# Two pairs of weight buffers change places in memory: the a22 quarter of the feed-forward projection

## The chip, the core and the metric

The kernel runs on one core of one Trainium2 chip. The metric is the device time of one execution in microseconds, the median over repeated runs.

## What is computed

A decoder block over 512 positions of 1024 channels, float32 throughout. The part that matters here is its last stage, a gated feed-forward layer with a short causal convolution (`h` is 512 x 1024, `w_ffn_in` 1024 x 5632, `w_ffn_out` 2816 x 1024):

```python
h = rmsnorm(x, norm2_g[l])
gu = h @ w_ffn_in[l]
g = causal_dwconv(gu[..., :D_FF], ffn_conv_w[l]) + ffn_conv_b[l]
x = x + (jax.nn.silu(g) * gu[..., D_FF:]) @ w_ffn_out[l]
```

Ahead of it stand the input projection, a gated short convolution, sparse attention, and the merge through `w_o`. The change touches none of them.

## The kernel before

**Split operands.** Each float32 operand of a large product is held as a high part (the value in TensorE's reduced float32 format) and a low part (the rest). A product is then three matmuls per 128 x 128 block of weights: high x high, high weights x low data, low weights x high data. The helper `dense` issues, for each block, the two with the high weights (lines 437 and 438), and after all blocks those with the low weights (line 440). So a high buffer is loaded into TensorE twice for each block, a low one once.

**The feed-forward stage.** The 2816 columns are taken two tiles of 128 at a time (f = 0, 2, ..., 20, 11 pairs), each for the gate half (n = 0) and the up half (n = 1) of `w_ffn_in`: 22 calls of `ff_forms` and `ff_pair`. Each is a 2 x 2 block product by Strassen's scheme in Winograd's form: seven products instead of eight. The weights of a call are cut in four quarters a11, a12, a21, a22, each 128 columns by 512 channels (four blocks of 128 x 128). The data is cut likewise, and its seven forms (B11, T4, B21, B22, T1, T3, T2) are made once and kept in `xf_h` and `xf_l`, 256 positions each. Every one of the seven products thus has four blocks and 4 x 3 = 12 matmuls of 256 moving columns, eight with high weights and four with low.

**Where the weights of the seven products lie.** a11 and a12 are kept in a ring of tiles `wh`/`wl` (named wh_s and wl_s in the profile). The four sums of quarters are made on VectorE and split into `sh`/`sl`. a22 itself has its own small tiles: `th` (high) and `tl` (low), 128 partitions x 2048 bytes, two buffers each, used by turns. `ff_forms` fills them with `dma_split` (lines 171 to 175): ScalarE writes the rounded raw weights into th and their negative into tl, and a transfer on the POOL queue adds the weights from the chip's main memory into tl. Only the product with the data form T4 uses a22 (`product(b45[:, lo], "a22", T4)`): eight matmuls with th, alternately on xf_h and xf_l, then four with tl on xf_h. It is written first of the seven.

Between the calls, the parts of the product with `w_ffn_out` (`pdn` in the profile, weights wh_d and wl_d from the same ring, data `ah` and `al`) are put in, with 512 moving columns. The last one is cut in two of 256 columns.

**What sets the order and the places.** A scheduler sets the order of the instructions on each engine. Places in a partition's memory follow from the order in which a pool's tiles are first named: each tag gets its buffers behind those of the tag before. In the pool `pw`, the line that the change touches names one tag ahead of a spacer of 192 bytes, `gap_w`. The other tags follow as `ff_forms` first names them. In the built program the places are, in bytes from the start of each partition:

| tile | before | past a multiple of 512 |
| --- | --- | --- |
| xf_h (28,672 bytes) | 37,152 | 288 |
| xf_l (28,672 bytes) | 65,824 | 288 |
| th, two buffers | 94,496 and 96,544 | 288 |
| gap_w | 98,592 | |
| tl, two buffers | 98,784 and 100,832 | 480 |
| sums, sh, sl (behind tl) | 102,880 to 135,648 | 480 |
| ah, al | 138,720 to 167,392 | 480 |
| ring wh, wl | 204,768 to 229,344 | 480 |

Each further block of weights lies 512 bytes on, each further block of data 7,168 (14 x 512).

Of the kernel before, what the change touches and what calls it, by code (L numbers as in the profile page):

```python
# [12 lines left out]
F32R = mybir.dt.float32r  # L13
# [5 lines left out]
P = 128  # L19
D = 1024  # L20
# [65 lines left out]
def tile_block(ctx: ExitStack, tc: tile.TileContext, xT, pos, par, par2, w_tok, w_a3, w_gate, w_ao, w_bo, w_o,  # L86
# [13 lines left out]
    def const(shape, name, dt=F32, pool=sb):  # L100
        return pool.tile(shape, dt, name=name, tag=name)
# [798 lines left out]
    xf_h = const([P, 4, 7, TH], "xf_h", F32R, px)  # L900
    xf_l = const([P, 4, 7, TH], "xf_l", F32R, px)
    pw = ctx.enter_context(tc.tile_pool(name="pw", bufs=1, side="left"))
    pw.tile([P, D // 2], F32R, name="th_", tag="th", bufs=2)
    const([P, 48], "gap_w", F32, pw)

    def x_forms(k, v):
# [283 lines left out]
```

## Time and profile before

| | |
| --- | --- |
| median of 3 runs | 697.33 us (697.29 to 697.89) |
| profiled execution, its own time | 696.92 us |
| its span, first to last instruction | 695.1 us |
| TensorE (PE) busy | 689.2 us, 99% |
| weight loads (PEld) busy, beside PE | 614.5 us, 88% |
| VectorE (DVE) busy | 511.7 us, 74% |
| ScalarE (ACT) busy | 436.7 us, 63% |
| GpSimd (POOL) busy | 248.7 us, 36% |

The profile is of one execution. A group's row gives line, engine, operation, the tile written and those read, the shape, the count, and behind the bar the busy time in us, the mean of one in ns, and the idle time of the engine ahead of them. Matmuls are pipelined: a record's duration runs from its issue to its modelled end and overlaps with the next. The pace of TensorE is the time from one start to the next.

### The profile page before, as it was taken

What the parts mean: (1) busy time and instruction counts of PE and PEld (TensorE: products, weight loads), DVE (VectorE), ACT (ScalarE), POOL (GpSimd) and SP (SyncE); (2) the same over time, 40 slices, a digit from 0 to 9 for tenths busy, and PEclk for the clock granted to TensorE, in tenths of its full rate; (3) what the DMA queues carried; (4) which work ended last, traced back from release to release, by engine and by line L of the source; (5) the groups of instructions that cost most, each with busy time, mean ns of one, the idle gap of its engine ahead of it and who ended that gap; (6) DMA issues with size and microseconds to landing.
All of it is one profiled execution on the core that took longest, in us unless ns stands there. A gap on an engine that the chain in (4) does not pass through costs nothing.

```text
span 695.1 us, 11268 instructions
## 1 busy us (share of the span) xinstructions
PE 689.2 (99%) x4111; PEld 614.5 (88%) x4111; DVE 511.7 (74%) x897; ACT 436.7 (63%) x776; POOL 248.7 (36%) x247
## 2 busy tenths in 40 slices
PE   9999999999999999999999999999999999999997
PEld 9999888887878888788889999999999999999986
DVE  6987886766566546475888999898787787877543
ACT  7635654878888866535776857665566655566530
POOL 4041443477788867462112212121122211112110
PEclk9999999999999999999999999999999999999999
DMA  8333686568666654563586977997877979775665
GB/s 268 113 98 122 170 194 145 132 240 237 222 222 228 195 169 124 193 229 118 130 198 160 219 192 167 245 218 180 215 173 180 210 172 227 174 175 112 132 137 152
DMA packets 57623, 124.87 MB, mean 180 GB/s; under 512 B 5344, under 2 KB 21088, under 8 KB 57568
## 3 DMA queue, kind: packets, MB, share of 16 engines
q1 hardware_dynamic: 35648, 79.39, 35.3%
q0 software_dynamic: 14848, 32.51, 27.4%
q10 hardware_dynamic: 7072, 12.26, 5.5%
q8 instruction: 32, 0.52, 0.3%
q14 instruction: 23, 0.19, 0.1%
HBM read 111.55 MB, written 12.58 MB: 179 GB/s over the span
## 4 chain that ended last, share of the span: by engine, by line
PE 95%; ACT 2%; DMA 1%; POOL 1%; DVE 1%; issue 0%; SPq 0%; ACTq 0%; POOLq 0%
PE p L438 10%; PE p L437 10%; PE p L440 10%; PE pdn L438 6%; PE pdn L437 6%; PE pdn L440 6%; PE pg L437 4%; PE pg L438 4%; PE pg L440 3%; PE pa L438 3%; PE pa L437 3%; PE pa L440 3%; PE po L438 2%; PE po L440 2%; PE po L437 2%; PE pj_s L269 2%
## 5 line engine op out<-in xcount | busy, mean ns | idle before, releaser
L437 PE MATMUL p<-xf_h,sh 128*128 128x256 f32 x336 | 80.6, 277 | 0.0
L438 PE MATMUL p<-xf_l,sh 128*128 128x256 f32 x336 | 80.5, 276 | 0.0
L175 POOL DMA_DIRECT2D wl_s<-in_w_ff_dram x22 | 19.6, 891 | 156.1 <-ACT wl_s L174 154.8
L438 PE MATMUL pdn<-al,wh_d 128*128 128x512 f32 (+1 forms) x176 | 68.5, 389 | 0.0
L437 PE MATMUL pdn<-ah,wh_d 128*128 128x512 f32 (+1 forms) x176 | 68.3, 389 | 0.0
L438 PEld LDWEIGHTS p<-xf_l,sh 128*128 128x128 f32 x336 | 63.1, 188 | 0.0
L437 PEld LDWEIGHTS p<-xf_h,sh 128*128 128x128 f32 x336 | 63.1, 188 | 0.0
L167 ACT ACTIVATE sh<-s 128x1024 fp32r<-128x1024 f32 x44 | 46.3, 1055 | 25.3 <-PE p L438 22.4
L168 DVE TENSOR_TENSOR sl<-s,sh 128x1024 fp32r<-128x1024 f32 x44 | 53.5, 1218 | 8.7 <-ACT sh L167 8.6
L173 ACT ACTIVATE wh_s<-wr_s 128x1024 fp32r<-128x1024 f32 x22 | 23.3, 1060 | 56.9 <-PE pdn L438 54.3
L750 POOL TENSOR_TENSOR tn_e<-tn_e,ph 128x512 fp32r<-128x512 f32 x40 | 51.2, 1294 | 16.2 <-ACT ph L749 16.0
L440 PE MATMUL p<-xf_h,sl 128*128 128x256 f32 x336 | 52.2, 277 | 0.0
L175 POOL DMA_DIRECT2D wl_d<-in_w_dn_dram x22 | 26.7, 1212 | 71.3 <-ACT wl_d L174 71.3
L437 PE MATMUL pg<-xg_h,wh_g 128*128 128x512 f32 x128 | 50.1, 392 | 0.0
L438 PE MATMUL pg<-xg_l,wh_g 128*128 128x512 f32 x128 | 50.1, 391 | 0.0
L440 PE MATMUL pdn<-ah,wl_d 128*128 128x512 f32 (+1 forms) x176 | 47.5, 388 | 0.0
L440 PEld LDWEIGHTS p<-xf_h,sl 128*128 128x128 f32 x336 | 44.7, 188 | 0.2
L1109 DVE TENSOR_TENSOR x<-x,pdn 128x512 f32<-128x512 f32 x47 | 32.0, 682 | 15.9 <-PE pdn L440 15.3
L150 POOL TENSOR_TENSOR wl_g<-wr_g,wh_g 128x1024 fp32r<-128x1024 f32 x16 | 38.5, 2405 | 10.4 <-ACT wh_g L148 9.7
L438 PE MATMUL p<-xf_l,wh_s 128*128 128x256 f32 x168 | 40.6, 277 | 0.0
L437 PE MATMUL p<-xf_h,wh_s 128*128 128x256 f32 x168 | 40.5, 277 | 0.0
L175 POOL DMA_DIRECT2D tl<-in_w_ff_dram x22 | 19.7, 894 | 57.3 <-ACT tl L174 49.7
(367 smaller groups left out, 2117.5 us busy)
## 6 DMA issues: line engine op xcount, KB each, us to landing
wr_s<-in_w_ff_dram SPq DMA_DIRECT2D x44, 512.0 KB, 5.0
wl_s<-in_w_ff_dram POOLq DMA_DIRECT2D x22, 512.0 KB, 7.8
wr_d<-in_w_dn_dram ACTq DMA_DIRECT2D x22, 512.0 KB, 8.3
wl_d<-in_w_dn_dram POOLq DMA_DIRECT2D x22, 512.0 KB, 9.0
wr_g<-in_w_gate_dram SPq DMA_DIRECT2D x16, 512.0 KB, 4.0
wr_a<-in_w_a_dram SPq DMA_DIRECT2D x12, 512.0 KB, 3.7
tl<-in_w_ff_dram POOLq DMA_DIRECT2D x22, 256.0 KB, 7.6
td_e<-e SPq DMA_DIRECT2D x16, 256.0 KB, 4.4
```

Source lines behind the costliest of these rows:

```text
L150: e.tensor_sub(lo[:, 0:n], raw[:, 0:n], hi[:, 0:n].bitcast(F32))
L167: hi = nc.scalar.activation(h, v, AF.Copy)
L168: nc.vector.tensor_sub(l, v, h.bitcast(F32))
L173: nc.scalar.activation(h, raw, AF.Copy)
L175: nc.gpsimd.dma_start(l if dst is None else dst, src, accum_op=ALU.add)
L269: nc.tensor.matmul(acc, xg_h[:, k, ts_], wh, start=k == 0, stop=False)
L437: ops.append(nc.tensor.matmul(acc, wh, xh, start=first and i == 0, stop=False))
L438: ops.append(nc.tensor.matmul(acc, wh, xl, start=False, stop=False))
L440: nc.tensor.matmul(acc, wl, xh, start=False, stop=last and i == len(units) - 1)
L750: nc.gpsimd.tensor_sub(pl, pt, ph.bitcast(F32))
L1109: nc.vector.tensor_add(xj, xj, acc)
```

## The change

One line names another tag ahead of the spacer, so that the low buffers are placed there and the high ones behind it:

```diff
     pw = ctx.enter_context(tc.tile_pool(name="pw", bufs=1, side="left"))
-    pw.tile([P, D // 2], F32R, name="th_", tag="th", bufs=2)
+    pw.tile([P, D // 2], F32R, name="tl_", tag="tl", bufs=2)
     const([P, 48], "gap_w", F32, pw)
```

In the built program th now lies at 98,784 and 100,832, and tl at 94,496 and 96,544. No other tile has another place. Every instruction, its order on its engine and its waits are the same as before.

## The prediction

> **What bounds the kernel now.** I read the page's busy table and its chain of waits first, then the waits of TensorE in the feed-forward stage, the only stage that uses the two buffers, then that stage's matmul groups, and at last single matmuls in order of time.
>
> ```profile
> span 695.1 us, 11268 instructions
> ...
> PE 689.2 (99%) x4111; PEld 614.5 (88%) x4111; DVE 511.7 (74%) x897; ACT 436.7 (63%) x776; POOL 248.7 (36%) x247
> ...
> PE 95%; ACT 2%; DMA 1%; POOL 1%; DVE 1%; issue 0%; SPq 0%; ACTq 0%; POOLq 0%
> ```
>
> TensorE is busy 99% of the span and the chain that ended last runs 95% through it. From 355 us to the end the list of waits for its weight loads has one row, and the list for its matmuls has none:
>
> ```profile
> PEld pdn7x L437 <- DVE x L1109: 0.3, 1, 0.3
> ```
>
> ```profile
> 440.00:690.00 250.00, 250.00 (x1731) 231.44 (x1731) 187.35 (x262) 138.54 (x181) 45.75 (x45) 1.00 0.78 179
> ```
>
> The second row gives the stretch, its length, and the busy time and count of PE, PEld, DVE, ACT and POOL: PE is busy 250.00 of 250.00 us at full clock. Nothing is waited for, so the stage lasts as long as its matmuls take to follow each other, and a nanosecond on the pace of one matmul reaches the end of the kernel. A nanosecond elsewhere reaches nothing.
>
> Within that stretch the groups of matmuls, one row per weight buffer (the last two numbers before the bar's end are busy us and mean ns of one):
>
> ```profile
> L437 PE MATMUL p<-xf_h,sh 128*128 128x256 f32 x240 | 57.4, 276 | 0.0
> ...
> L440 PE MATMUL p<-xf_h,sl 128*128 128x256 f32 x240 | 37.0, 276 | 0.0
> L437 PE MATMUL p<-xf_h,wh_s 128*128 128x256 f32 x120 | 28.7, 276 | 0.0
> ...
> L440 PE MATMUL p<-xf_h,wl_s 128*128 128x256 f32 x120 | 18.5, 276 | 0.0
> L438 PE MATMUL p<-xf_l,th 128*128 128x256 f32 x60 | 14.9, 282 | 0.0
> L437 PE MATMUL p<-xf_h,th 128*128 128x256 f32 x60 | 14.9, 281 | 0.0
> L440 PE MATMUL p<-xf_h,tl 128*128 128x256 f32 x60 | 9.2, 276 | 0.0
> ```
>
> All have one shape. Every weight buffer gives 276 ns, tl too, and th alone gives 281 and 282. These durations overlap, so the pace is read from starts. One a22 product and the product behind it, in order of time (start us, duration us):
>
> ```profile
> 488.98 0.28 PE L437 MATMUL p<-xf_h,th 128*128 128x256 f32 x1
> ...
> 489.81 0.28 PE L438 MATMUL p<-xf_l,th 128*128 128x256 f32 x1
> 489.93 0.62 PE L440 MATMUL p<-xf_h,tl 128*128 128x256 f32 x4
> 490.38 0.28 PE L437 MATMUL p<-xf_h,wh_s 128*128 128x256 f32 x1
> ...
> 491.18 0.28 PE L438 MATMUL p<-xf_l,wh_s 128*128 128x256 f32 x1
> 491.29 0.62 PE L440 MATMUL p<-xf_h,wl_s 128*128 128x256 f32 x4
> 491.74 0.28 PE L437 MATMUL p<-xf_h,wh_s 128*128 128x256 f32 x1
> ```
>
> The eight th matmuls take 489.93 - 488.98 = 0.95 us, 119 ns each. The four tl matmuls take 0.45 us, 113 each. Eight with wh_s take 0.91 and four with wl_s 0.45, again 113 each. So th costs about 0.04 us per product more than another buffer would, 5 ns a matmul, the same 5 ns as between 276 and 281 or 282. The slowness ends with the last th matmul: tl, behind it, is at pace at once.
>
> **Why th.** The addresses of the built program offer a reason. Both moving tiles, xf_h and xf_l, lie 288 bytes past a multiple of 512 bytes in their partition. So do both th buffers. Every other weight buffer of the stage, tl, sh, sl, wh and wl, lies 480 past one, because gap_w (192 bytes) stands behind th and ahead of the rest. A weight load streams while the matmul before it streams its moving operand, so equal offsets could make the two meet in the same part of the memory. One other place tests this, the last w_dn product, which is cut into two of 256 columns. There a moving tile (ah, al) and the weights (wh_d, wl_d) all lie 480 past a multiple of 512, as they do in the products of 512 columns ahead of it:
>
> ```profile
> 688.34 0.39 PE L437 MATMUL pdn<-ah,wh_d 128*128 128x512 f32 x1
> ...
> 689.02 0.39 PE L438 MATMUL pdn<-al,wh_d 128*128 128x512 f32 x1
> 689.25 0.62 PE L440 MATMUL pdn<-ah,wl_d 128*128 128x512 f32 x2
> 689.70 0.28 PE L437 MATMUL pdn<-ah,wh_d 128*128 128x256 f32 x1
> 689.81 0.28 PE L438 MATMUL pdn<-al,wh_d 128*128 128x256 f32 x1
> 689.93 0.28 PE L437 MATMUL pdn<-ah,wh_d 128*128 128x256 f32 x1
> 690.05 0.28 PE L438 MATMUL pdn<-al,wh_d 128*128 128x256 f32 x1
> 690.17 0.40 PE L440 MATMUL pdn<-ah,wl_d 128*128 128x256 f32 x2
> ```
>
> At 512 columns four take 689.25 - 688.34 = 0.91 us, 227 each, which is twice 113.5: no penalty. At 256 columns, from the second on, three take 690.17 - 689.81 = 0.36 us, 120 each: th's pace, with other buffers far from th. Equal offsets and 256 columns is what the two places share. It is an inference from two places, not a demonstration.
>
> **The change part by part.** It removes, adds and moves no instruction: the instructions and their waits stand in the same order on every engine. Four buffers get other addresses. th moves to 98,784 and 100,832 (480 past a multiple of 512), tl to 94,496 and 96,544 (288 past one). There are 22 such products (2 halves for each of 11 pairs of tiles).
>
> First term, th leaves the offset of its moving tiles: eight matmuls at 113.5 in place of 119, -0.04 us a product. Second term, tl takes that offset: four matmuls per product, all with xf_h. Its cost is not in the trace. From below it is nothing, since tl now runs at 113 beside the same xf_h and could go on so. From above it is th's own penalty on each, 4 x 5 = 0.02 us, or 4 x 6.5 = 0.026 at the 120 ns of the last product. A gain from the move is excluded: tl is already at the common pace. I take 0.02, because the equal offset is the nearest condition for which rows exist, and both rows of it pay. Net: -0.04 + 0.02 = -0.02 us a product.
>
> The count has its own bounds. Where the program takes several products by turns, the pace is 119 for buffers at any offset:
>
> ```profile
> 408.34 0.28 PE L437 MATMUL p<-xf_h,sh 128*128 128x256 f32 x1
> ...
> 409.17 0.28 PE L438 MATMUL p<-xf_l,sh 128*128 128x256 f32 x1
> 409.29 0.63 PE L440 MATMUL p<-xf_h,sl 128*128 128x256 f32 x4
> ```
>
> Eight sh matmuls take 0.95 us here, so a better offset would bring th nothing in such a stretch. Such stretches all lie ahead of 440 us; the means of 276 behind it leave no room for one. Behind 440 us are 60 / 4 = 15 products, which gain for certain if any do. So 15 to 22 products x 0.02 = 0.3 to 0.44 us, and I take 0.4. As the stage has no waits, all of it arrives at the end.
>
> Third term, the writers of the buffers. ScalarE writes th and tl, and a transfer from the POOL queue adds into tl. These are covered by lead time:
>
> ```profile
> 370.22 0.92 POOL L175 DMA_DIRECT2D tl<-in_w_ff_dram  x1 [1.24 <-ACT tl L174]
> ...
> 478.01 0.86 POOL L175 DMA_DIRECT2D tl<-in_w_ff_dram  x1
> ```
>
> ```profile
> 380.25 0.62 PE L440 MATMUL p<-xf_h,tl 128*128 128x256 f32 x4
> ...
> 504.95 0.62 PE L440 MATMUL p<-xf_h,tl 128*128 128x256 f32 x4
> ```
>
> ```profile
> DMA to landing us min/median/max: 3.8/7.6/9.7
> ```
>
> Issue to first use is 10 us in the tightest pair I looked at (370.22 to 380.25) and 27 us in the later ones (478.01 to 504.95). The slowest landing of all 22 takes 9.7 and the median 7.6. The transfer has the same size and comes from the same place, so I cost the move at zero. Without that cover each late microsecond would stand on TensorE.
>
> **A rule that speaks against it.** The Trainium skill, page "SBUF — State Buffer", section "Who interferes with whom", gives TensorE two independent read ports, one for the moving operand and one for weight loads, and says that it never waits on anyone. By that rule both terms are zero and the sum is 697.3. The trace does not agree: 281 and 282 against 276 for one buffer among equals. The page "TensorE: Matmul & The Clock Gate", section "LDWEIGHTS (loading the stationary operand)", puts a load of 128 columns at 128 / 1.2, an estimate of 107 ns. That would leave a load little room beside 113 ns and much beside 227, which would fit the missing penalty at 512 columns. No run here shows a load's bare time.
>
> **The sum.** The profiled execution took 696.92 us, 0.41 under the median of 697.33 shown for three runs. It becomes 696.92 - 0.4 = 696.5, and the median 697.33 - 0.4 = 696.9.
>
> **The rivals.**
>
> *Only the pairing with xf_l hurts.* xf_l lies at 65,824 to 94,496 and th right behind it, and both could sit in one block of the memory. tl meets only xf_h, so its term is zero, and the gain is 15 to 22 times 0.04, or 0.6 to 0.9: about 696.5. For it: xf_l is used in no product with tl. Against it: the xf_h matmuls of th are as slow as the xf_l ones (281 and 282), and the last w_dn product pays with tiles some 50,000 bytes apart.
>
> *The slowness is not of the place.* It belongs to the a22 product itself (its column T4, or its position behind a w_dn part), and th keeps it: 697.3. For it: th is used in that product alone, so row and product can't be separated in this trace. Against it: tl runs the same column of xf_h at 113. (The rule of the Trainium skill's page "SBUF — State Buffer" would have this case.) The same time results if the penalty is per new weight slice, since th brings four new slices a product and tl also four.
>
> *Slower: the pace of the mixed stretches takes hold behind tl.* tl ends its product. If its late weight loads leave the weight loads behind the matmuls, the 72 matmuls of the pair's other six products (12 each) follow at 119 in place of 113.5, 5 ns each. Over the 15 products behind 440 us that is 15 x 72 x 5 ns = 5.4 us, less 0.4: 702.3. It decides for slower once it holds 1.8 us, a third of those matmuls. For it: that pace exists and lasts for 0.95 us and more without any equal offset. Against it: behind th, which is eight slow loads in a row, the pace is back with the first tl.
>
> **How the numbers follow.** Forecast (th freed, tl pays) 0.66; xf_l alone 0.12; place without effect 0.14; slower by the mixed pace 0.05; something of a size that no row explains 0.03. The likeliest case gives 696.9, with its own range of 696.6 to 697.3 from the bounds and the spread of the runs (697.29 to 697.89). The range to hold 8 in 10 runs from 696.3, which takes in the xf_l case, to 697.7, which takes in no effect and that spread. 0.2% of the time is 1.39 us, about what a measurement can tell from no change. Even a whole recovery (22 x 0.04 = 0.9) stays inside it. So "same" holds the first three cases nearly whole, 0.89; slower 0.06; faster 0.05, since no row has 1.4 us to give.
>
> **What would show it.** In the changed profile, behind 440 us: th at 276 and tl at about 281 (forecast); both at 276 (xf_l alone); th still at 281 and tl at 276 (place without effect). Eight th matmuls in 0.91 us and four tl in 0.47 or more. sh, wh_s and sl stay at 276; if they go to 279 or more there, it is the mixed pace. TensorE must still show no wait behind 440 us. A span that moves by over a microsecond with those groups unchanged would mean that the time is set somewhere I haven't looked, and the forecast wrong.

## The result and the profile after

The changed kernel takes 702.08 us (median of 6 runs, 701.37 to 702.73), the kernel before 697.31 beside it (6 runs, 695.81 to 698.02). The ratio is 1.0070, with a 95% interval of 1.0057 to 1.0083. It is slower by 4.8 us, outside the predicted range of 696.3 to 697.7, and where the third rival, "Slower: the pace of the mixed stretches takes hold behind tl", had put it (702.3). The profiled execution took 701.78 us (span 700.0), against 696.92 (span 695.1).

The page of the kernel after, its span, busy times and chain of waits:

```profile
span 700.0 us, 11268 instructions
...
PE 694.4 (99%) x4111; PEld 620.6 (89%) x4111; DVE 512.7 (73%) x897; ACT 436.9 (62%) x776; POOL 248.5 (35%) x247
...
PE 90%; DMA 3%; ACT 3%; POOL 2%; DVE 1%; issue 1%; SPq 0%; ACTq 0%; POOLq 0%
```

Instructions and counts are those of before. PE is busy 5.2 us longer in a span that is 4.9 us longer. The waits of its weight loads from 355 us to the end are the one row of before, word for word (0.3 us at pdn7x), so the chain's smaller share of PE doesn't come from a wait in the stage. The stretch from 440 to 690 us is still all PE at full clock (columns as in the prediction):

```profile
440.00:690.00 250.00, 250.00 (x1707) 232.27 (x1706) 185.09 (x257) 138.94 (x181) 45.76 (x45) 1.00 0.77 175
```

The count says it: 1707 matmuls in the same 250 us, where before had 1731. No wait came, and the clock is the same. The matmuls follow each other more slowly. The groups of that stretch, kernel after:

```profile
L437 PE MATMUL p<-xf_h,sh 128*128 128x256 f32 x240 | 59.1, 279 | 0.0
...
L440 PE MATMUL p<-xf_h,sl 128*128 128x256 f32 x240 | 38.0, 280 | 0.0
...
L437 PE MATMUL p<-xf_h,wh_s 128*128 128x256 f32 x120 | 29.6, 279 | 0.0
...
L438 PE MATMUL p<-xf_l,th 128*128 128x256 f32 x60 | 14.9, 280 | 0.0
...
L440 PE MATMUL p<-xf_h,tl 128*128 128x256 f32 x60 | 9.7, 284 | 0.0
```

Buffers whose places did not change (sh, sl, wh_s) went from 276 to 279 or 280. th is at 280 and tl at 284. One call in order of time, kernel after (start us, duration us):

```profile
443.56 0.28 PE L437 MATMUL p<-xf_h,th 128*128 128x256 f32 x1
...
444.50 0.65 PE L440 MATMUL p<-xf_h,tl 128*128 128x256 f32 x4
444.98 0.28 PE L437 MATMUL p<-xf_h,wh_s 128*128 128x256 f32 x1
...
446.40 0.28 PE L437 MATMUL p<-xf_h,wh_s 128*128 128x256 f32 x1
...
447.81 0.28 PE L437 MATMUL p<-xf_h,sh 128*128 128x256 f32 x1
...
695.50 0.39 PE L437 MATMUL pdn7x<-ah,wh_d 128*128 128x256 f32 x1
```

Eight th take 444.50 - 443.56 = 0.94 us, 118 ns each, four tl 0.48 us, 120 each. The 24 matmuls with wh_s and wl_s take 447.81 - 444.98 = 2.83 us, 118 each, where before has 113.3 (1.36 us for 12). The same two ends in the kernel before:

```profile
443.90 0.28 PE L437 MATMUL p<-xf_h,th 128*128 128x256 f32 x1
...
690.64 0.39 PE L437 MATMUL pdn7x<-ah,wh_d 128*128 128x256 f32 x1
```

From the first th to the first pdn7x matmul: 690.64 - 443.90 = 246.74 us before, 695.50 - 443.56 = 251.94 after, so +5.20 us. At the first of these points the kernel after is 0.34 us ahead, so 5.20 - 0.34 = 4.86 is the whole difference of the spans. The parts of the 5.20: 15 calls x 72 matmuls of the other six products x (117.8 - 113.3, the means over all their starts) = 4.9 us; 15 x (0.48 - 0.45) = 0.45 for tl; 15 x (0.94 - 0.95) = -0.15 for th. Sum 5.2.

### The profile page after: what moved, and what is told of

Same layout as the page of the kernel before. It is cut to its first block, busy times and chain, and to the rows that moved or that the text cites. A ratio compares the mean times of both kernels' runs of the same rounds, so it can differ in the third digit from the quotient of the medians.

```text
span 700.0 us, 11268 instructions
## 1 busy us (share of the span) xinstructions
PE 694.4 (99%) x4111; PEld 620.6 (89%) x4111; DVE 512.7 (73%) x897; ACT 436.9 (62%) x776; POOL 248.5 (35%) x247
## 4 chain that ended last, share of the span: by engine, by line
PE 90%; DMA 3%; ACT 3%; POOL 2%; DVE 1%; issue 1%; SPq 0%; ACTq 0%; POOLq 0%
PE p L440 10%; PE p L437 10%; PE p L438 10%; PE pdn L438 6%; PE pdn L437 6%; PE pdn L440 6%; PE pg L438 3%; PE pg L437 3%; PE pg L440 3%; PE pa L438 3%; PE pa L437 3%; PE pa L440 3%; PE po L438 2%; PE po L437 2%; PE po L440 2%; PE pj_s L269 2%
## 5 line engine op out<-in xcount | busy, mean ns | idle before, releaser
L437 PE MATMUL p<-xf_h,sh 128*128 128x256 f32 x336 | 82.4, 279 | 0.0
L438 PE MATMUL p<-xf_l,sh 128*128 128x256 f32 x336 | 82.4, 279 | 0.0
```

The lines of the kernel that those rows point to most:

```text
L437: ops.append(nc.tensor.matmul(acc, wh, xh, start=first and i == 0, stop=False))
L438: ops.append(nc.tensor.matmul(acc, wh, xl, start=False, stop=False))
```

## Theories and experiments

A shift of two buffers slowed others that didn't move. I read all starts of the 256-column matmuls in both traces (the series below, in ns from one start to the next, are worked out so). Behind a w_dn part the kernel before shows 116, 117, 120, 121, 117, 117, 120, 121 over its eight th matmuls (each to within 2 ns), then 113, 113, 114, 113 and so on to the next w_dn part, in all 15 calls behind 440 us. The kernel after shows 118, 118, 120, 118, 117, 119, 117, 118 (th), then 121, 120, 124, 117 (tl), then 118 to the next w_dn part, also in all 15. So two lasting paces exist, 113 and 118, at the same places, with the same buffers.

- **Theory A.** The passage from a w_dn part (512 columns) leaves TensorE in the 118 pace, in the kernel before too. th's eight weight loads at the data's offset (288) cost a toll of their own, and end the 118 pace. After the change nothing ends it.
- **Theory B** (the rival as predicted). tl's loads at the data's offset set the 118 pace off.

Each diff is against the kernel after, but for two that are said to be against the kernel before. Unless said otherwise a kernel computes everything, and its groups are those of 440 to 690 us. "Before" is the median of the kernel before on the same chip. "Stage time" is the time from the first th matmul behind 440 us to the first pdn7x matmul of the profiled execution: 246.74 us in the kernel before, 251.94 in the kernel after.

### No a22 buffer at the data's offset

```diff
-    pw.tile([P, D // 2], F32R, name="tl_", tag="tl", bufs=2)
     const([P, 48], "gap_w", F32, pw)
```

The spacer stands ahead of both, so th and tl lie 480 past a multiple of 512.

> The spacer stands ahead of both tags: th and tl both lie 480 past a multiple of 512, so neither has the offset of xf_h and xf_l (288). Theory A (th at the data's offset brings the stream back from 118 to 113 ns after each w_dn part, and without it the slow pace stays): th, tl, sh, wh_s all near 118 behind 440 us, time 702.1 less the toll of tl (15 to 22 times 0.025), so 701.5 to 701.8. Rival B (tl at the data's offset is what holds the slow pace): all buffers at 113 behind 440 us, time 697.3 less th's old toll of 0.6 to 0.9, so about 696.5.

702.66 us (701.54 to 703.49, 4 runs; before 696.94), ratio 1.0084 (1.0069 to 1.0099). Groups:

```profile
L437 PE MATMUL p<-xf_h,sh 128*128 128x256 f32 x240 | 59.2, 280 | 0.0
...
L437 PE MATMUL p<-xf_h,wh_s 128*128 128x256 f32 x120 | 29.6, 280 | 0.0
```

The 118 pace is there with no buffer of weights at the data's offset. B falls: tl isn't its cause. A had foreseen this pace, but its time, 701.5 to 701.8, was too low. The stage time is 251.94 us (444.86 to 696.80), the same as in the kernel after: in the 118 pace tl's toll is only 11 ns a call (its four take 482 ns there and 471 here), and the w_dn parts take as much longer (24 matmuls at a mean of 228.2 ns in place of 227.8).

### Both a22 buffers at the data's offset

Against the kernel before:

```diff
     pw.tile([P, D // 2], F32R, name="th_", tag="th", bufs=2)
+    pw.tile([P, D // 2], F32R, name="tl_", tag="tl", bufs=2)
     const([P, 48], "gap_w", F32, pw)
```

> The spacer stands behind both tags: th and tl both lie 288 past a multiple of 512. Theory A: th brings the pace back, tl only pays its own toll of about 0.025 us in 22 products, time 697.3 + 0.4 to 0.6 = 697.8, sh and wh_s at 113. Rival B: tl holds the slow pace as in the changed kernel, time 702 to 703, sh and wh_s at 118.

697.87 us (696.60 to 699.06, 10 runs; before 696.94), ratio 1.0014 (1.0004 to 1.0023). Groups:

```profile
L437 PE MATMUL p<-xf_h,sh 128*128 128x256 f32 x240 | 57.4, 276 | 0.0
...
L437 PE MATMUL p<-xf_h,th 128*128 128x256 f32 x60 | 14.9, 281 | 0.0
...
L440 PE MATMUL p<-xf_h,tl 128*128 128x256 f32 x60 | 9.6, 283 | 0.0
```

tl has the offset that it has in the kernel after, and the 113 pace is back. th at 288 is what brings it. tl pays its toll: its starts are 120, 120, 120 and 120 or 121 in all 15 calls, 15 x 4 x 6.7 = 0.4 us. The stage time is 247.14 us (444.59 to 691.73), 0.40 above the kernel before: tl's toll and nothing else. With the seven other products of this kind it is up to 0.6 of the 0.9 us that this kernel is slower.

### th at the data's offset in every other call

The two buffers of th get tags of their own. The gate half's lies at 288, the up half's at 480.

```diff
-    pw.tile([P, D // 2], F32R, name="tl_", tag="tl", bufs=2)
+    pw.tile([P, D // 2], F32R, name="th_", tag="th0", bufs=1)
...
-        h = pw.tile([P, HALF_D], F32R, name=f"th{nm}", tag="th", bufs=2)
+        h = pw.tile([P, HALF_D], F32R, name=f"th{nm}", tag=f"th{n}", bufs=1)
```

> th's two buffers become two tags: the one for the gate half (n=0) lies at 288, the one for the up half (n=1) at 480, and tl at 480. Theory A: within one run every gate half runs at 113 behind its th and every up half at 118, time about half way, 699 to 700. Rival B: no tl at 288, so both halves at 113, time 696.5 to 697.

700.07 us (699.81 to 700.55, 4 runs; before 696.94), ratio 1.0048 (1.0033 to 1.0063). A gate half and the up half behind it, in order of time:

```profile
460.92 0.28 PE L437 MATMUL p<-xf_h,wh_s 128*128 128x256 f32 x1
...
462.28 0.28 PE L437 MATMUL p<-xf_h,wh_s 128*128 128x256 f32 x1
...
475.96 0.28 PE L437 MATMUL p<-xf_h,wh_s 128*128 128x256 f32 x1
...
477.38 0.28 PE L437 MATMUL p<-xf_h,wh_s 128*128 128x256 f32 x1
```

Twelve matmuls with the same ring of weights take 462.28 - 460.92 = 1.36 us in the gate half, 113 each, and 477.38 - 475.96 = 1.42 in the up half, 118 each. All 7 gate halves behind 440 us hold 113 and all 8 up halves 118. The stage time is 249.5 us (444.15 to 693.66), 2.8 above the kernel before, and 8 of 15 calls make 8/15 x 5.20 = 2.8. In the kernel before both halves hold 113 and in the kernel after both hold 118, so it isn't the half that matters: within one execution, th's place decides for the 72 matmuls behind it.

### How many loads, and where they must stand

First, only blocks 0 and 1 of the gate half's th at 288 (four loads), the up half's all at 480. A gap of 192 bytes inside the buffer moves blocks 2 and 3:

```diff
+            h = pw.tile([P, 640], F32R, name=f"th{nm}", tag="th0", bufs=1)[:, 0:608].rearrange("p (a c) -> p a c", a=2)[:, :, 0:256]
```

> For the gate half (n=0) blocks 0 and 1 of th lie at 288 and blocks 2 and 3 at 480; for the up half (n=1) all of th at 480; tl at 480. So behind each w_dn part the gate half has four loads at the data's offset instead of eight, and the up half none. Theory A-place (equal offset right behind the w_dn part is enough): gate halves at 113 after th, up halves at 118, time 699.5 to 700. Theory A-count (all eight are needed, which would also explain why tl's four do not help): gate halves stay at 118 too, time 702 to 702.8.

702.64 us (702.62 and 702.66; before 696.74), ratio 1.0085 (1.0056 to 1.0114): all groups at 279 or 280, as with none. The starts of a gate half's th are 115, 119, 119, 120, 112, 119, 117, 118, and then 118. These eight take 939 ns, the eight of an up half, with no load at the data's offset, 944 or 945. Four loads cost nothing there and end nothing.

Then six loads (three blocks) in the gate half, and all eight in the up half. The write of the gate half's th becomes two ScalarE instructions:

```diff
+        if n == 0:
+            nc.scalar.activation(h[:, 0:384], a22[:, 0:384], AF.Copy)
+            nc.scalar.activation(h[:, 432:560], a22[:, 384:512], AF.Copy)
```

> Between the four loads that did not bring the pace back and the eight that do: in the gate half blocks 0 to 2 of th (six loads) at 288 and block 3 at 480, in the up half all of th at 288, tl at 480. If six are enough: both halves at 113, 697.0 to 697.6 (toll 0.1 us smaller). If not: gate halves at 118 and up halves at 113, about 700.

700.13 us (698.71 to 702.05, 8 runs; before 697.20), ratio 1.0040 (1.0029 to 1.0051). An up half and the gate half behind it:

```profile
448.10 0.28 PE L437 MATMUL p<-xf_h,wh_s 128*128 128x256 f32 x1
...
449.46 0.28 PE L437 MATMUL p<-xf_h,wh_s 128*128 128x256 f32 x1
...
463.14 0.28 PE L437 MATMUL p<-xf_h,wh_s 128*128 128x256 f32 x1
...
464.56 0.28 PE L437 MATMUL p<-xf_h,wh_s 128*128 128x256 f32 x1
```

With eight loads the next twelve take 1.36 us (113), with six 1.42 (118), in all 8 up halves and all 7 gate halves. The gate half begins 116, 118, 120, 120, 117, 118, as the gate half of the kernel with one th at 288 does (there 120, 120 follow, and 113). The start is the same, and the last two loads make the difference. The stage time is 249.17 us (446.70 to 695.87), 2.43 above the kernel before, and 7/15 x 5.20 = 2.43.

Last, the places of the kernel before, with the a22 product written sixth of the seven (against the kernel before):

```diff
-        product(b45[:, lo], "a22", T4)
...
+        product(b45[:, lo], "a22", T4)
```

> The places are those of the kernel before (th at 288, tl at 480), but the a22 product is written sixth of the seven instead of first, so it no longer stands behind the w_dn part. Theory A-anywhere (eight loads at the data's offset bring the pace back wherever they stand): behind 440 us the first five products of a half at 118, a22 pays its toll, the last at 113; five sevenths of the slow pace, 700.5 to 701.5. Theory A-place (they only work right behind the w_dn part): the last product too stays at 118, 702 to 703.

700.58 us (700.30 to 701.04, 3 runs; before 697.20), ratio 1.0052 (1.0026 to 1.0079). One call:

```profile
458.86 0.28 PE L437 MATMUL p<-xf_h,wh_s 128*128 128x256 f32 x1
...
465.93 0.28 PE L437 MATMUL p<-xf_h,th 128*128 128x256 f32 x1
...
467.33 0.28 PE L437 MATMUL p<-xf_h,sh 128*128 128x256 f32 x1
...
468.69 0.39 PE L437 MATMUL pdn<-ah,wh_d 128*128 128x512 f32 x1
```

Five products, 60 matmuls, take 465.93 - 458.86 = 7.07 us, 118 each. After th the 12 left take 1.36, 113 each. So the 118 pace is there in the kernel before's own places as soon as th doesn't come first, it lasts for 60 matmuls, and th's loads end it in the middle of a call too: in 14 of the 15 calls behind 440 us. In the 15th (th at 450.53) the starts are 121, 120, 124, 118, 117, 121, 120, 120, and 118 stays. The eight loads don't always do it.

### What the entry hangs on: the w_dn part's offsets

Theory A left open why a w_dn part leaves the 118 pace. In the kernel before its data (ah, al) and weights (wh_d, wl_d) have equal offsets. A first theory A1 said that this is why. A spacer moves ah and al away from them, with th and tl both at 480 as in the first experiment:

```diff
-    pw.tile([P, D // 2], F32R, name="tl_", tag="tl", bufs=2)
     const([P, 48], "gap_w", F32, pw)
...
+    const([P, 48], "gap_a", F32, pf)
```

> As with both th and tl at 480, and besides the data of the w_dn product, ah and al, moved from 480 to 288 by a spacer ahead of them, so that the weights wh_d and wl_d (480) no longer have their data's offset. Theory A1 (the w_dn part makes the stream slow because its weights and data have equal offsets): no slow pace is entered, 113 everywhere behind 440 us, time 697.3 less th's toll (0.8) and less part of the stretches ahead of 440 us (up to 1.5), so 695 to 696.5. Theory A2 (the passage from 512 to 256 columns makes it slow, whatever the offsets): 118 behind 440 us as with both at 480, time 701.5 to 701.8.

697.08 us (median of 10 runs; nine at 696.08 to 698.34, one at 703.38; before 696.94), ratio 1.0007 (0.9985 to 1.0029). Groups:

```profile
L437 PE MATMUL pdn<-ah,wh_d 128*128 128x512 f32 x155 | 60.6, 391 | 0.0
L438 PE MATMUL p<-xf_l,sh 128*128 128x256 f32 x240 | 57.4, 276 | 0.0
...
L438 PE MATMUL p<-xf_l,th 128*128 128x256 f32 x60 | 14.3, 276 | 0.0
```

All 256-column groups are at 276, without any toll, as A1 wants. But the w_dn matmuls pay: their starts go round 226, 229 or 230, 231 or 232, mean 228.9, against 227 at equal offsets. The time is above A1's 695 to 696.5, in part for this. And one run of ten lost the whole 6 us. Two other distances of ah and al from the weights, 32 and 96 bytes, by the size of the same spacer (8 and 24 floats in place of 48):

> th and tl both at 480 (64 on from xf_h, xf_l), and ah, al moved 32 bytes down, so that wh_d, wl_d stand 32 bytes on from their data. With them 64 on, the stream left the w_dn parts at 113 but those parts themselves ran at 229 to 230 in place of 227. If the entry into the slow pace needs equal offsets in the w_dn part: 113 behind 440 us, pdn at 227 to 230, 695 to 698. If not: 118, 702 to 703.

> As before, with ah, al moved 96 bytes down, so that wh_d, wl_d stand 96 on from their data. If the entry into the slow pace needs equal offsets in the w_dn part: 113 behind 440 us, 695 to 698. If not: 118, 702 to 703.

32 bytes: 700.20 us (699.58 to 701.17, 5 runs; before 697.57), ratio 1.0040 (1.0018 to 1.0061). 96 bytes: 704.74 (703.27 to 706.21, 2 runs), ratio 1.0112 (1.0053 to 1.0171). The groups of the first, then of the second:

```profile
L437 PE MATMUL pdn<-ah,wh_d 128*128 128x512 f32 x153 | 60.5, 395 | 0.0
L437 PE MATMUL p<-xf_h,sh 128*128 128x256 f32 x240 | 57.4, 276 | 0.0
```

```profile
L437 PE MATMUL p<-xf_h,sh 128*128 128x256 f32 x240 | 59.2, 280 | 0.0
...
L437 PE MATMUL pdn<-ah,wh_d 128*128 128x512 f32 x146 | 57.9, 397 | 0.0
```

At 32 bytes the stage enters 113, but each w_dn matmul pays (starts of 232 and 235), more than the 227 to 230 that was expected, and the time is 2.2 us above the expected 698. At 96 it enters 118, and they pay about as much (mean start to start 234 ns), so that the time is above the expected 703 too. Unequal offsets don't guarantee the 113 pace: A1 falls.

Then the two together, th at 288 in the gate half only, and ah and al moved by the 48 floats:

> Two placements joined: ah and al at 288, so that the w_dn part leaves the stream at 113, and th of the gate halves alone at 288 (th of the up halves and tl at 480), so that a slow pace that starts for another reason is ended once a pair. If both do what they did alone: 113 behind 440 us, half of th's toll (0.4), the w_dn parts at 229 instead of 227 (1.0 us), the pace back at 113 from the second pair on: 696 to 697, within 0.2% of the kernel before. If they don't add, 698 to 701.

701.25 us (699.98 to 702.06, 8 runs; before 697.03), ratio 1.0056 (1.0041 to 1.0071). A miss: 696 to 697 was expected. A gate half that held 113 (its th at 459.07), and the next gate half (th at 489.14):

```profile
460.48 0.28 PE L437 MATMUL p<-xf_h,wh_s 128*128 128x256 f32 x1
...
461.83 0.28 PE L437 MATMUL p<-xf_h,wh_s 128*128 128x256 f32 x1
...
490.57 0.28 PE L437 MATMUL p<-xf_h,wh_s 128*128 128x256 f32 x1
...
491.99 0.28 PE L437 MATMUL p<-xf_h,wh_s 128*128 128x256 f32 x1
```

Twelve take 1.35 us in the one and 1.42 in the other, with the same places. Three of the seven gate halves start 113, 119 or 120, 120 (already in the 113 pace, th paying its toll) and hold 113; the other four end at 118 in spite of eight loads. Behind w_dn matmuls that go round three durations, the pace entered differs from call to call. Behind w_dn parts at equal offsets it was 118 in every call behind 440 us of the kernels in which xf_h and xf_l lie 192 or 64 bytes from the weights and no th at the data's offset stands first. That the phase in which the last w_dn matmul ends decides is what these series suggest; no run set that phase by itself.

### The distance between weights and moving data

In these kernels gap_w stands ahead of th and tl as in the first experiment, and gap_x and gap_w are sized to move xf_h and xf_l, while all weights stay at 480. Distances between the two: 256, 128, 64, 96 and 160 bytes (the kernel before has 192). The first of the five diffs:

```diff
-    const([P, 80], "gap_x", F32, px)
+    const([P, 64], "gap_x", F32, px)
...
-    pw.tile([P, D // 2], F32R, name="tl_", tag="tl", bufs=2)
-    const([P, 48], "gap_w", F32, pw)
+    const([P, 64], "gap_w", F32, pw)
```

> xf_h and xf_l moved to 224 past a multiple of 512, all weights at 480: a distance of 256 bytes in place of 192, no buffer at the data's offset. If the slow pace is tied to the distance of 192, behind 440 us all groups run at 113: 695.5 to 696.5. If any unequal distance lets it stay: 118 behind 440 us, 701.5 to 703.

> xf_h and xf_l at 352, all weights at 480: a distance of 128. As for 256: 113 and 695.5 to 696.5 if the slow pace is tied to 192, 118 and 701.5 to 703 if not. If the memory repeats every 128 bytes, it is as with equal offsets: 119 to 121 everywhere, 703 to 706.

> xf_h and xf_l at 416, all weights at 480: a distance of 64. 113 and 695.5 to 696.5 if the slow pace is tied to 192, 118 and 701.5 to 703 if not. If the memory repeats every 128 bytes, 64 and 192 are the same and it is as with both th and tl at 480: 702.7.

> xf_h and xf_l moved so that the weights (all at 480) stand 96 bytes on from them, counted within 128 bytes. Distances of 0 and of 64 have been tried; if the memory repeats every 128 bytes, 32 and 96 are the two left on the allocation's grid. If the slow pace at 118 belongs to 64 alone: 113 behind 440 us, no toll, 695 to 696. If it comes with any unequal distance: 118, 702 to 703.

> xf_h and xf_l moved so that the weights stand 32 bytes on from them, counted within 128 bytes (160 in full). If the slow pace belongs to 64 alone: 113, 695 to 696. If it comes with any unequal distance: 118, 702 to 703. If 32 is near enough to equal: 119 to 121, up to 707.

Measured, two runs each, with the time from one 256-column start to the next:

| distance, bytes | past a multiple of 128 | us | ratio to before (95%) | ns a matmul behind 440 us |
| --- | --- | --- | --- | --- |
| 256 | 0 | 706.97 | 1.0147 (1.0117 to 1.0176) | 120 |
| 128 | 0 | 706.82 | 1.0145 (1.0115 to 1.0174) | 120 |
| 64 | 64 | 702.24 | 1.0079 (1.0050 to 1.0108) | 118 |
| 96 | 96 | 704.38 | 1.0107 (1.0062 to 1.0151) | 118.7 |
| 160 | 32 | 707.29 | 1.0148 (1.0115 to 1.0182) | 120 |

Two of the five fit no case of their expectation: 256 bytes gave 120 ns, not 113 or 118, and 96 gave 118.7 and a time above the expected 703 us. 64 came out as one of its cases. So did 128 and 160 (both as equal offsets), 0.8 and 0.3 us above the times given.

One product of the kernel with 256 bytes, whose twelve matmuls take 449.08 - 447.64 = 1.44 us, 120 each:

```profile
447.64 0.28 PE L437 MATMUL p<-xf_h,wh_s 128*128 128x256 f32 x1
...
449.08 0.28 PE L437 MATMUL p<-xf_h,wh_s 128*128 128x256 f32 x1
```

256 and 128 bytes cost the same as equal offsets do, and 64 behaves as 192: places count by their remainder of 128, not of 512. th's toll of 120 ns now stands on every matmul. With 64 bytes, the groups of 360 to 400 us, ahead of the first w_dn part, and of 405 to 425, behind it:

```profile
L437 PE MATMUL p<-xf_h,sh 128*128 128x256 f32 x48 | 11.5, 276 | 0.0
```

```profile
L437 PE MATMUL p<-xf_h,sh 128*128 128x256 f32 x24 | 5.9, 281 | 0.0
```

The first row holds the whole products, from 374 us on. The mixed ones ahead of them, from 358 us, directly behind the 512 columns of the w_o part, run at 118 in this kernel, before and after alike. So here the 118 pace comes with a part of 512 columns. It isn't the only way in. The kernel with ah and al at 288 runs sh at 279 from 360 to 400 us, ahead of any w_dn part, and flips from 113 to 118 in the middle of a product:

```profile
424.66 0.28 PE L437 MATMUL p<-xf_h,wh_s 128*128 128x256 f32 x1
...
425.57 0.66 PE L440 MATMUL p<-xf_h,wl_s 128*128 128x256 f32 x4
426.07 0.28 PE L437 MATMUL p<-xf_h,wh_s 128*128 128x256 f32 x1
...
427.01 0.63 PE L440 MATMUL p<-xf_h,wl_s 128*128 128x256 f32 x4
```

Eight take 425.57 - 424.66 = 0.91 us, the four with wl_s 0.50 in place of 0.45 (their starts are 148, 117, 117 and 120 ns apart), and the eight behind take 427.01 - 426.07 = 0.94. One gap 35 ns too long goes with the flip. Neither the cause of that gap nor what TensorE holds between matmuls is shown by a record.

Nor is a part of 512 columns a sure way to 118, or th the only way out of it. Ahead of 440 us, in the kernel after, two w_dn matmuls at 417.42 stand between sh matmuls: ahead of them the starts are 117 to 119, behind them 114, 113, 113, 114. In the kernel before the same two, at 417.69, lead from 113 to 118. And in the kernel with 64 bytes a start-to-start time of 180 ns (at 425.84) stands where the pace goes from 118 to 113. So a break in the stream can set either pace. What th's eight loads do is to set it to 113 at the start of nearly every call.

## Why the prediction was wrong, by its own steps

**"What bounds the kernel now": right.** TensorE stays busy at full clock and nothing waits. "A nanosecond on the pace of one matmul reaches the end of the kernel" is just what happened: 4.5 ns on 1080 matmuls.

**"Why th": half right.** Equal offsets do cost 120 ns at 256 columns and nothing at 512, as inferred from two places; the kernels with 256 and 128 bytes show it for all buffers. The remainder that counts is that of 128 bytes, and 32 bytes apart costs as much.

**"First term, th leaves the offset ... -0.04 us a product": the step that failed.** It took th's eight loads only as a cost. The trace of before had the sign of the rest in rows that I quoted and read the other way: "The slowness ends with the last th matmul: tl, behind it, is at pace at once." th is slow there mostly because the stream comes to it at 118 (949 ns over its eight in before, 944 in after, so the toll is under 1 ns each), and without th the stream would have stayed at 118. Moving th brought -0.01 us a product behind 440 us (0.94 in place of 0.95), not -0.04. The sum had no term for the rest: 4.5 ns on each of the 72 matmuls behind th, +0.32 us a call. Where no w_dn part stands ahead, the term came true. The second pair of tiles, kernel after:

```profile
378.91 0.28 PE L437 MATMUL p<-xf_h,th 128*128 128x256 f32 x1
...
379.82 0.64 PE L440 MATMUL p<-xf_h,tl 128*128 128x256 f32 x4
380.30 0.28 PE L437 MATMUL p<-xf_h,wh_s 128*128 128x256 f32 x1
```

Eight th in 0.91 us, 113 each, where the kernel before takes 0.95 (379.30 to 380.25).

**"Second term, tl takes that offset": right, 0.02 taken.** Four tl in 0.48 us in these rows, 120 each, in place of 0.45: 0.03 a product, its upper bound.

**"Such stretches all lie ahead of 440 us": a true reading that was given the wrong cause.** I took the 119 of the stretches with mixed products for a property of mixing. It is the lasting 118 pace: the eight sh matmuls that I read as 119 have starts of 116 to 119, mean 117.9, and their product isn't taken by turns with another. The trace of before even shows the pace begin and end there. Behind w_dn matmuls at 404.50, the 46 matmuls from 406.34 to 411.76 take 5.42 us, 118 each. Then comes an a22 product, kernel before:

```profile
411.76 0.28 PE L437 MATMUL p<-xf_h,th 128*128 128x256 f32 x1
...
412.71 0.62 PE L440 MATMUL p<-xf_h,tl 128*128 128x256 f32 x4
413.16 0.28 PE L437 MATMUL p<-xf_h,wh_s 128*128 128x256 f32 x1
```

Four tl take 0.45 us, and 113 holds to 417.69. In the kernel after the same product (th at 411.30) leaves 118 as it is. In the kernel before the 118 pace is missing behind 440 us only because th ends it at the start of every call.

**"Third term, the writers": right.** No new wait appeared behind 440 us.

**The rivals.** "Slower: the pace of the mixed stretches takes hold behind tl" had the right size (702.3, against 702.08) and the right stretch, with a chance of 0.05. Its trigger, tl's late loads, is refuted: with tl at 480 as well the loss is the same. The sign that the prediction gave for this rival, sh and wh_s at 279 or more, is the one that came. The argument against it, "behind th, which is eight slow loads in a row, the pace is back with the first tl", was the mechanism itself, seen as a reassurance. "Only the pairing with xf_l hurts" falls by tl at 284 on xf_h alone. "The slowness is not of the place" was nearly right for th's own rows behind a w_dn part (118 in place of 119), but falls by the second pair. With it falls, for the pace of this kernel, the rule that the prediction took from the Trainium skill's page "SBUF — State Buffer", section "Who interferes with whom", of two independent read ports and a TensorE that never waits on anyone: places alone move the kernel from 697 to 707 us here. What it is that weights and data share isn't shown.

**The range.** 696.3 to 697.7 held every case in which each buffer's pace hangs on its own place. It left out that a pace can outlast its cause, though rows at 119 without equal offsets were quoted and no term explained them. They were the reason for a wider range.

**Open.** Why eight loads at the data's offset end the 118 pace, and six don't; why eight fail in some calls (one of 15 with the late a22 product, four of seven with ah and al moved; three of these five start 120 or 121, 120, 124 or 125 within the first four). tl's four loads in the kernel after also start 121, 120, 124 (or 120, 120, 125) in all 15 calls, so for tl the number of loads and the moment at which they come aren't told apart. The runs of the kernel before spread from 695.8 to 699.3 over all comparisons, which the stretches ahead of 440 us in one or the other pace could explain; no second profile of it is there to show this. In other kernels some of it lies there: the profiled runs with one th and with six loads have stage times of 249.5 and 249.2 us, but take 699.95 and 702.05, as the second comes to the stage's start 2.55 us later. No kernel tried is faster than the kernel before.

## What to carry to other kernels

A slow instruction in a saturated stream may be doing something: before taking its cost away, compare the pace on both sides of it, and ask which of the two would last without it. When unchanged rows show a pace that no theory of yours explains, price the case that it spreads to the whole stage, and let the range reach there. Where TensorE is the bound, treat the offset of weights and moving data within 128 bytes as a parameter to be measured on the whole kernel.

## What the runs showed of the hardware

- With 256 moving columns of split float32 and a new weight load for each matmul, the time from start to start hangs on the distance of weights and data modulo 128 bytes: 0 or 32 give 120 ns, 96 about 118.7, and 64 gives 113.3 or 117.8.
- Of those two, one lasts until something shifts it: 60 matmuls and more at 118 (7.07 us) with nothing waited for, at full clock, in the same places in which 113 is held elsewhere in the same execution. A w_dn part of 24 matmuls of 512 columns at equal offsets left it at 118 (all 15 calls of the kernel after), eight loads at equal offsets right behind such a part put it at 113 (all 15 calls of the kernel before), and shorter breaks set either: two matmuls of 512 columns led to 113 in one kernel and to 118 in the other, a gap 35 ns too long stood at a flip to 118, one 62 ns too long at a flip to 113.
- With 512 columns the order is another: 227 ns at equal offsets, 228.9 at 64 bytes, 232 and 235 by turns at 32, 234 at 96. Equal offsets are best there and among the worst at 256.
